# Strassen's algorithm for nine of eleven K-block pairs of the FFN down projection

## The chip, the core and the metric

The kernel runs on one core of a Trainium2 chip. The metric is the device time of one execution in microseconds (us); the kernel before took 1108.36 us, the median of three runs (1108.16 to 1108.46). Five engines matter: TensorE (PE, with its weight loads as PEld) multiplies, VectorE (DVE), ScalarE (ACT) and GpSimd (POOL) work element by element, SyncE (SP) issues the DMAs. SBUF is the on-chip memory of 128 partitions; TensorE writes its results to PSUM, eight banks of 128 x 512 fp32.

## The reference

Two layers of an encoder on 256 tokens, D = 1024, in fp32. Each layer has an FFN, an attention and gating block, and another FFN. Cut to what matters here:

```
def swiglu(x, w_gate, w_up, w_down):
    return (jax.nn.silu(x @ w_gate) * (x @ w_up)) @ w_down

for l in range(DEPTH):                       # DEPTH = 2
    x = x + 0.5 * swiglu(rms_norm(x, ffn1_norm[l]), ffn1_w_gate[l], ffn1_w_up[l], ffn1_w_down[l])
    ...                                      # attention, gates, w_out
    x = x + 0.5 * swiglu(rms_norm(x, ffn2_norm[l]), ffn2_w_gate[l], ffn2_w_up[l], ffn2_w_down[l])
```

The hidden width is 2816, so the down projection multiplies 256 x 2816 by 2816 x 1024, four times in all.

## The kernel before

**Matmuls in three parts.** TensorE is given fp32 numbers in a rounded form (fp32r). So that nothing is lost, each operand is split into a rounded part and the rest: `hi = round(a)` by a copy on ScalarE, `lo = a - hi` by a subtraction on VectorE (`split_to`, lines 176 and 177; for weights the same in `load`, lines 133 and 134, into wh and wl). A product of two blocks is then three matmuls of 512 columns, `three` (lines 162 to 164): hi by hi, hi by lo, lo by hi. This text calls three such matmuls one product.

**Weights.** All weights come through one helper. `load` takes a `raw` buffer of 128 x 1024 (4 of them), issues a DMA of 512 KB on the SP queue, and splits the buffer into wh and wl (RING = 6 slots each). A slot comes free when TensorE has used it in its last product, and a raw buffer when both halves of the split have read it.

**The FFN** (`ffn`) is two stages. Gate/up: eleven chunks c of 256 hidden columns; each chunk loads four pieces of weights and, for each of the two token halves t (128 tokens each), `project` makes eight products into one PSUM bank; Silu on ScalarE (line 323) and a product on VectorE (hh, line 325) make 128 x 256 of the hidden layer. `turn` transposes it on TensorE in 128 x 128 blocks (line 305), and splits the transposed blocks of a chunk from PSUM into hi and lo. `turn` isn't called at once: `defer` and `tick` keep a count of products, and a deferred step is issued when its due count comes (H_LAG = 7.9 for `turn`), or earlier if someone needs it.

Down: `out_rows` runs over the K blocks (128 hidden columns each, 22 in all, two to a chunk). Each loads one row block of w_down, 128 x 1024, and makes four products, one for each token half t and column half d, into four PSUM banks that accumulate over all of K (tags pt, po, and sc twice). So a pair of K blocks, one chunk c, costs eight products. The last four row blocks are one group: there the order is t, then d, then the block, so that banks end one after the other; as each ends, line 292 adds half of it to x, and `after` defers the next norm's transposes of that quarter by NORM_LAG = 4 products. The norm's power (rsqrt, line 168) runs on GpSimd.

**Order.** TensorE's order is the order in which the program is written, with the deferred steps in their places. The order on the other engines is a planner's: it models the program in time ahead of the launch and takes on each engine what is ready, earlier program steps first. On the chip each engine then takes its own list in order.

GpSimd also works in the attention stage: line 443 scales 128 x 512 scores, line 537 adds a mask to a bias.

Of the kernel before, what the change touches and what calls it, by code (L numbers as in the profile page):

```python
# [11 lines left out]
F32 = mybir.dt.float32  # L12
F32R = mybir.dt.float32r
I32 = mybir.dt.int32
BF16 = mybir.dt.bfloat16
AF = mybir.ActivationFunctionType
ALU = mybir.AluOpType
# [4 lines left out]
P = 128  # L22
# [3 lines left out]
FF = 2816  # L26
T = S // P
KD = D // P
FC = 256
NFC = FF // FC  # L30
# [11 lines left out]
RAW = 4  # L42
# [4 lines left out]
FMAX = 3.0e38  # L47
IN_W = 4352
HEAD = 128


@with_exitstack
def hybrid_encoder(ctx, tc, x, w_gu1, w_d1, w_in, b_gate, qk_gain, rpb, sink, t5,
                   w_bna, w_bsw, w_out, w_gu2, w_d2, c_mask, c_hot, c_band, out):
    nc = tc.nc

    const = ctx.enter_context(tc.tile_pool(name="const", bufs=1))
    ring = ctx.enter_context(tc.tile_pool(name="ring", bufs=1))
    act = ctx.enter_context(tc.tile_pool(name="act", bufs=1))
    small = ctx.enter_context(tc.tile_pool(name="small", bufs=4))  # L60
    ps_g = ctx.enter_context(tc.tile_pool(name="ps_g", bufs=2, space=PSUM))
    ps_acc = ctx.enter_context(tc.tile_pool(name="ps_acc", bufs=1, space=PSUM))
    ps_tp = ctx.enter_context(tc.tile_pool(name="ps_tp", bufs=2, space=PSUM))
# [6 lines left out]

    wide = act.tile([P, HEAD + D], F32, name="x0", tag="x0")
    gain = wide[:, :3 * L * KD].rearrange("p (n k) -> p n k", n=3 * L)
    xs = [wide[:, HEAD:], act.tile([P, D], F32, name="x1", tag="x1")]

    def fetch(t, h):
        if (t, h) == (0, 0):
            nc.sync.dma_start(wide[:, :HEAD + 512], x[:P, :HEAD + 512])
        else:
            nc.sync.dma_start(xs[t][:, h * 512:(h + 1) * 512],
                              x[t * P:(t + 1) * P, HEAD + h * 512:HEAD + (h + 1) * 512])  # L80

    fetch(0, 0)

    ident = const.tile([P, P], F32, name="ident")
# [33 lines left out]
    def linked(engine, emit):  # L118
        with ExitStack() as order:
            if engine in chain:  # L120
                order.enter_context(tc.issue_after(chain[engine].ins))
            inst = emit()
        if chain:
            chain[engine] = inst
        return inst

    def load(src, nk, n, tag="raw"):
        raw = ring.tile([P, 2, 512], F32, name="raw", tag="raw", bufs=RAW)
        wh = ring.tile([P, 2, 512], F32R, name="wh", tag="wh", bufs=RING)
        wl = ring.tile([P, 2, 512], F32R, name="wl", tag="wl", bufs=RING)  # L130
        r, h, lo = (w[:, :nk, :n] for w in (raw, wh, wl))
        nc.sync.dma_start(r, src)
        linked("act", lambda: nc.scalar.activation(h, r, AF.Copy))  # L133
        linked("dve", lambda: nc.vector.tensor_tensor(lo, r, h.bitcast(F32), ALU.subtract))  # L134
        return wh, wl

    def columns(w, l, c0, n, nk=KD):
        return [load(w[l, 2 * i * P:(2 * i + 2) * P, c0:c0 + n].rearrange("(k p) n -> p k n", p=P), 2, n)
                for i in range(nk // 2)]

    def rows(w, l, k):
        return load(w[l, k * P:(k + 1) * P, :].rearrange("p (h n) -> p h n", h=2), 2, 512)
# [4 lines left out]
    def defer(lag, key, fn):  # L147
        later.append((now[0] + lag, len(later), key, fn))
        later.sort(key=lambda e: e[0])

    def need(*keys):
        for e in [e for e in later if e[2] in keys]:
            later.remove(e)
            e[3]()

    def tick(cost):
        now[0] += cost
        while later and later[0][0] <= now[0]:
            later.pop(0)[3]()

    def three(ps, xh, xl, wh, wl, first, last):
        nc.tensor.matmul(ps, xh, wh, start=first, stop=False)  # L162
        nc.tensor.matmul(ps, xh, wl, start=False, stop=False)  # L163
        nc.tensor.matmul(ps, xl, wh, start=False, stop=last)  # L164
# [10 lines left out]
    def split_to(hi, lo, src):  # L175
        linked("act", lambda: nc.scalar.activation(hi, src, AF.Copy))
        linked("dve", lambda: nc.vector.tensor_tensor(lo, src, hi.bitcast(F32), ALU.subtract))  # L177
# [39 lines left out]
    def opening(w, l):  # L217
        def piece(i, c=0):
            return load(w[l, 2 * i * P:(2 * i + 2) * P, c * 512:(c + 1) * 512].rearrange("(k p) n -> p k n", p=P),
                        2, 512)  # L220
# [43 lines left out]
    def project(t, pieces, n):  # L264
        ps = ps_g.tile([P, 512], F32, name="g", tag="g")
        for k in range(KD):
            need(("norm", t, k // 4))
            xh, xl = xT[t]
            wh, wl = pieces[k // 2]
            three(ps[:, :n], xh[:, k, :], xl[:, k, :], wh[:, k % 2, :n], wl[:, k % 2, :n], k == 0, k == KD - 1)  # L270
            tick(n / 512)
        return ps

    ACC = ((("pt", 1), ("po", 1)), (("sc", 2), ("sc", 2)))

    def out_rows(get, nk, w, l, groups, scale, after):
        acc = [[ps_acc.tile([P, 512], F32, name="acc", tag=tag, bufs=n) for tag, n in pair] for pair in ACC]
        k0 = 0
        for g in (*[1] * (nk - sum(groups)), *groups):
            pieces = [(k, *rows(w, l, k)) for k in range(k0, k0 + g)]  # L280
            k0 += g
            order = [(d, p) for d in range(2) for p in pieces]
            if k0 < nk:
                order.sort(key=lambda e: e[1][0])
            for t in range(T):
                for d, (k, wh, wl) in order:
                    xh, xl = get(t, k)
                    three(acc[t][d], xh, xl, wh[:, d, :], wl[:, d, :], k == 0, k == nk - 1)
                    tick(1)
                    if k == nk - 1:  # L290
                        xd = xs[t][:, d * 512:(d + 1) * 512]
                        nc.vector.scalar_tensor_tensor(xd, acc[t][d], scale, xd, op0=ALU.mult, op1=ALU.add)  # L292
                        after(t, d)

    def ffn(l, n, w_gu, w_d, after):
        with tc.tile_pool(name="ffn", bufs=1) as fp:
            hs = {}
            tps = {}

            def turn(c, t, hh):  # L300
                if t == 0:
                    tps[c] = ps_tp.tile([P, 2, 2, P], F32, name="tp", tag="tp")
                tp = tps[c]
                for i in range(2):
                    nc.tensor.transpose(tp[:, i, t, :], hh[:, i * P:(i + 1) * P], ident)  # L305
                if t == T - 1:
                    hi = fp.tile([P, 2, 2, P], F32R, name="hi", tag="hi", bufs=NFC)
                    lo = fp.tile([P, 2, 2, P], F32R, name="lo", tag="lo", bufs=NFC)
                    split_to(hi, lo, tp)
                    hs[c] = (hi, lo)  # L310

            for c in range(NFC):
                first = n == 0 and c == 0
                if first:
                    both, second = opening(w_gu, l)
                elif n == 0 and c == 1:
                    pieces = second
                else:
                    pieces = columns(w_gu, l, c * 512, 512)
                for t in range(T):  # L320
                    ps = both[t] if first else project(t, pieces, 512)
                    sg = fp.tile([P, FC], F32, name="sg", tag="sg", bufs=2)
                    nc.scalar.activation(sg, ps[:, :FC], AF.Silu, scale=rstd[t])  # L323
                    hh = fp.tile([P, FC], F32, name="hh", tag="hh", bufs=2)
                    nc.vector.scalar_tensor_tensor(hh, ps[:, FC:], rstd[t], sg, op0=ALU.mult, op1=ALU.mult)  # L325
                    defer(H_LAG, ("h", c), lambda c=c, t=t, hh=hh: turn(c, t, hh))

            def get(t, k):
                need(("h", k // 2))
                return [h[:, k % 2, t, :] for h in hs[k // 2]]  # L330

            out_rows(get, FF // P, w_d, l, (4,), 0.5, after)

    vec_d = dram.tile([NH, 511], F32, name="vec_d")

# [13 lines left out]
    def mix(l, n, after):  # L349
        with tc.tile_pool(name="mix", bufs=1) as mp:  # L350
# [204 lines left out]
            for token in ORDER.split():  # L555
                if token[0] == "a":
                    it, h = next(heads)
# [51 lines left out]
            def get(t, k):  # L609
                need(("merge", t, k // 4))  # L610
                return [m[:, k, :] for m in mT[t]]

            out_rows(get, KD, w_out, l, (4, 4), 0.5, after)

    def store(t, d):
        cols = slice(d * 512, (d + 1) * 512)
# [6 lines left out]
    for l in range(L):  # L623
        ffn(l, 3 * l, w_gu1, w_d1, soon(3 * l + 1))
        mix(l, 3 * l + 1, soon(3 * l + 2))
        ffn(l, 3 * l + 2, w_gu2, w_d2, soon(3 * l + 3) if l + 1 < L else store)
# [67 lines left out]
```

## Time and profile before

| | |
|---|---|
| median of three runs | 1108.36 us |
| the profiled execution | 1108.37 us, of which the span from the first to the last instruction is 1106.5 us |
| TensorE, busy | 1096.3 us, 99% |
| VectorE, busy | 700.5 us, 63% |
| ScalarE, busy | 600.4 us, 54% |
| GpSimd, busy | 103.9 us, 9% |
| granted clock of TensorE | 0.999 on average |

Lines of the profile name an instruction by its source line, engine and operation, then what it writes and reads by the program's names (`wl<-raw,wh`), then shapes as partitions x elements, the number of such instructions, their busy time in us and the mean duration of one in ns, and the idle time of the engine ahead of them with what ended it. A matmul's recorded duration overlaps its neighbours', so a pace is read from starts. Engines' lists of semaphore waits carry a q (DVEq, POOLq). The view of one line or one tile gives shortest, median and longest duration. A timeline gives start and duration in us from the start of the span.

### The profile page before, as it was taken

The numbers are of one execution on the slowest core, as the hardware profiler recorded it, in microseconds if no ns is written. First come the engines' busy times: TensorE is split into PE (matmuls) and PEld (weight loads), VectorE is DVE, ScalarE is ACT, GpSimd is POOL, SyncE is SP. The second block draws the span as 40 slices with busy tenths as digits, with TensorE's granted clock in tenths as the row PEclk, the third lists the DMA queues.
The fourth block names the chain that finished last, engine by engine and source line by source line (L and its number), as shares of the span: only waits on it lengthen the run. The fifth ranks groups of instructions, "written<-read, shape, count | busy, mean of one in ns | idle before, by whom it ended". The sixth has DMA issues, their size and how long they took to land.

```text
span 1106.5 us, 14361 instructions
## 1 busy us (share of the span) xinstructions
PE 1096.3 (99%) x5223; PEld 906.1 (82%) x5223; DVE 700.5 (63%) x987; ACT 600.4 (54%) x914; POOL 103.9 (9%) x101
## 2 busy tenths in 40 slices
PE   9999999999999999999999999999999999999998
PEld 7788888888888888888888888888888888888887
DVE  6655644888887655564475565457888767555542
ACT  6544543788764554454364544347877546454431
POOL 1000000143420000000000000003434000000000
PEclk9999999999999999999999999999999999999999
DMA  7665565765655556556656556647565555646561
GB/s 238 227 188 192 175 212 165 214 189 150 192 183 154 186 175 193 187 176 213 181 156 209 168 187 208 194 119 240 183 190 184 166 171 163 209 161 195 203 192 57
DMA packets 95399, 203.23 MB, mean 184 GB/s; under 512 B 7200, under 2 KB 13376, under 8 KB 95328
## 3 DMA queue, kind: packets, MB, share of 16 engines
q1 hardware_dynamic: 95104, 202.17, 57.7%
q8 instruction: 41, 0.67, 0.3%
q0 software_dynamic: 224, 0.14, 0.1%
q14 instruction: 30, 0.25, 0.1%
HBM read 201.22 MB, written 1.06 MB: 183 GB/s over the span
## 4 chain that ended last, share of the span: by engine, by line
PE 90%; DVE 4%; ACT 3%; issue 2%; DMA 1%; ACTq 0%; DVEq 0%
PE g L162 19%; PE g L164 19%; PE g L163 18%; PE acc L164 9%; PE acc L162 9%; PE acc L163 9%; PE tp L305 2%; DVE wl L134 2%; ACT wh L133 1%; PE tp L193 1%; PE pt L451 1%; PE sc L430 1%; PE g L229 1%; PE po L465 1%; PE br L163 1%
## 5 line engine op out<-in xcount | busy, mean ns | idle before, releaser
L134 DVE TENSOR_TENSOR wl<-raw,wh 128x1024 fp32r<-128x1024 f32 (+1 forms) x368 | 447.0, 1219 | 196.5 <-ACT wh L133 182.7
L133 ACT ACTIVATE wh<-raw 128x1024 fp32r<-128x1024 f32 (+1 forms) x368 | 383.6, 1049 | 209.9 <-PE acc L164 125.2
L162 PE MATMUL g<-wh,xh 128*128 128x512 f32 (+1 forms) x976 | 390.2, 400 | 0.0
L164 PE MATMUL g<-wh,xl 128*128 128x512 f32 (+1 forms) x976 | 379.4, 389 | 0.0
L163 PE MATMUL g<-wl,xh 128*128 128x512 f32 (+1 forms) x976 | 377.8, 387 | 0.4 <-DVE wl L134 0.4
L164 PEld LDWEIGHTS g<-wh,xl 128*128 128x128 f32 x976 | 183.4, 188 | 40.5 <-DVE xl L177 1.3
L163 PEld LDWEIGHTS g<-wl,xh 128*128 128x128 f32 x976 | 184.2, 189 | 31.9 <-DVE wl L134 0.8
L162 PEld LDWEIGHTS g<-wh,xh 128*128 128x128 f32 x976 | 183.7, 188 | 31.5 <-issue 0.9
L323 ACT ACTIVATE sg<-g,rs_y 128x256 f32<-128x256 f32 x88 | 41.7, 474 | 181.6 <-PE g L164 181.4
L162 PE MATMUL acc<-wh,hi 128*128 128x512 f32 x352 | 138.5, 394 | 0.0
L164 PE MATMUL acc<-wh,lo 128*128 128x512 f32 x352 | 137.3, 390 | 0.0
L163 PE MATMUL acc<-wl,hi 128*128 128x512 f32 x352 | 137.1, 389 | 0.0
L325 DVE SCALAR_TENSOR_TENSOR hh<-g,rs_y,sg 128x256 f32<-128x256 f32 x88 | 42.3, 481 | 139.4 <-ACT sg L323 139.4
L164 PEld LDWEIGHTS acc<-wh,lo 128*128 128x128 f32 x352 | 66.1, 188 | 13.9
L163 PEld LDWEIGHTS acc<-wl,hi 128*128 128x128 f32 x352 | 66.2, 188 | 13.4
L162 PEld LDWEIGHTS acc<-wh,hi 128*128 128x128 f32 x352 | 66.1, 188 | 13.3
L168 POOL TENSOR_TENSOR rs_y<-ms,mhalf 128x1 f32<-128x1 f32 x12 | 7.2, 600 | 654.6 <-DVE ms L214 647.4
L443 POOL TENSOR_TENSOR S<-S,sm 128x512 f32<-128x512 f32 x32 | 37.1, 1159 | 71.7 <-DVE sm L442 45.3
L436 ACT ACTIVATE S<-S,mx 128x256 f32<-128x256 f32 x64 | 31.8, 498 | 7.5 <-DVE mx L433 7.4
L305 PEld LDWEIGHTS tp<-ident,hh 128*128 128x128 f32 x176 | 24.6, 140 | 11.3
L292 DVE SCALAR_TENSOR_TENSOR x<-acc,x 128x512 f32<-128x512 f32 x24 | 16.6, 690 | 26.6 <-PE acc L164 26.6
L305 PE MATMUL tp<-ident,hh 128*128 128x128 f32 x176 | 33.3, 271 | 0.0
(133 smaller groups left out, 925.8 us busy)
## 6 DMA issues: line engine op xcount, KB each, us to landing
raw<-in_w_gu SPq DMA_DIRECT2D x176, 512.0 KB, 4.6
raw<-in_w_d SPq DMA_DIRECT2D x88, 512.0 KB, 3.7
raw<-in_w_in SPq DMA_DIRECT2D x64, 512.0 KB, 4.5
raw<-in_w_out SPq DMA_DIRECT2D x16, 512.0 KB, 3.5
bb<-in_b_gate SPq DMA_DIRECT2D x16, 256.0 KB, 3.5
raw<-in_w_bsw SPq DMA_DIRECT2D x8, 512.0 KB, 4.1
raw<-in_w_bna SPq DMA_DIRECT2D x8, 512.0 KB, 3.5
t5b<-vec_d SPq DMA_DIRECT2D x16, 192.0 KB, 3.5
```

What stands on the lines that cost most here:

```text
L133: linked("act", lambda: nc.scalar.activation(h, r, AF.Copy))
L134: linked("dve", lambda: nc.vector.tensor_tensor(lo, r, h.bitcast(F32), ALU.subtract))
L162: nc.tensor.matmul(ps, xh, wh, start=first, stop=False)
L163: nc.tensor.matmul(ps, xh, wl, start=False, stop=False)
L164: nc.tensor.matmul(ps, xl, wh, start=False, stop=last)
L193: nc.tensor.transpose(tp[:, i, :], xs[t][:, k * P:(k + 1) * P], ident)
L292: nc.vector.scalar_tensor_tensor(xd, acc[t][d], scale, xd, op0=ALU.mult, op1=ALU.add)
L305: nc.tensor.transpose(tp[:, i, t, :], hh[:, i * P:(i + 1) * P], ident)
L323: nc.scalar.activation(sg, ps[:, :FC], AF.Silu, scale=rstd[t])
L325: nc.vector.scalar_tensor_tensor(hh, ps[:, FC:], rstd[t], sg, op0=ALU.mult, op1=ALU.mult)
L436: nc.scalar.activation(S_[:, t, :], S_[:, t, :], AF.Exp, bias=mx[:, t:t + 1], scale=-1.0, accum_out=sm[:, t:t + 1])
L443: nc.gpsimd.tensor_tensor(S_, S_, sm.unsqueeze(2).to_broadcast([P, T, S]), ALU.mult)
```

## The change

The 256 tokens are two halves, the 1024 output columns are two halves, and a pair of K blocks is two halves: for each pair the down projection is a 2 x 2 by 2 x 2 block product. The change computes it for the first nine pairs (NS = 9) with seven block products, by the Winograd form of Strassen's algorithm, and keeps the last two pairs (four row blocks) as they were.

- `turn` copies the four transposed blocks of a chunk from PSUM to SBUF on ScalarE (tile a), makes three sums and differences that the algorithm needs and one on the way to them on GpSimd (128 x 128 each), and splits seven blocks from SBUF where four were split from PSUM. The last two chunks stay as before.
- `sevens(c)` loads the two row blocks of a pair, the second into a buffer of its own (`odd`, 3 of them). It splits one corner of 512 columns, the whole second row block, and two tiles u and v of 1024 columns with the differences of weight blocks; those are four subtractions of 128 x 512 on GpSimd, where the second of u feeds the first of v, which feeds the second. u, v and a share four buffers (`sums`). Corner, low, us and vs are the seven right-hand operands; low, us and vs take ring slots, the corner has buffers of its own.
- `products()` accumulates the seven products over the nine pairs in seven PSUM banks. Those of products 2, 3 and 4 go on as accumulators of three of the four output blocks; 1, 5, 6 and 7 are combined by `plus` on VectorE into the parts that the blocks share, three of which GpSimd adds to x and one VectorE.
- `out_rows` then runs over the last four row blocks only, with the accumulators it is given, and takes a new bank for the one that it isn't given.

Cut to its core (`parts` is the splitting half of `load`; `load` itself, and the call of `out_rows` for w_out, do the same as before):

```
+NS = 9
...
+    def parts(r, nk=2, n=512):
         wh = ring.tile([P, 2, 512], F32R, name="wh", tag="wh", bufs=RING)
         wl = ring.tile([P, 2, 512], F32R, name="wl", tag="wl", bufs=RING)
+        split_to(wh[:, :nk, :n], wl[:, :nk, :n], r)
+        return wh, wl
...
             for t in range(T):
                 for d, (k, wh, wl) in order:
+                    first = acc[t][d] is None
+                    if first:
+                        acc[t][d] = out_bank(t, d)
                     xh, xl = get(t, k)
-                    three(acc[t][d], xh, xl, wh[:, d, :], wl[:, d, :], k == 0, k == nk - 1)
+                    three(acc[t][d], xh, xl, wh[:, d, :], wl[:, d, :], first, k == nk - 1)
...
+                if m == 7:
+                    a = fp.tile([P, 8, P], F32, name="a", tag="sums", bufs=4)
+                    nc.scalar.activation(a[:, :4, :], tp, AF.Copy)
+                    for to, x, y, op in ((4, 0, 3, ALU.add), (6, 1, 0, ALU.subtract), (5, 4, 1, ALU.subtract),
+                                         (7, 2, 5, ALU.subtract)):
+                        nc.gpsimd.tensor_tensor(a[:, to, :], a[:, x, :], a[:, y, :], op)
+                    split_to(hi, lo, a[:, 1:, :])
+                else:
                     split_to(hi, lo, tp)
...
+            def sevens(c):
+                r0 = ring.tile([P, 2, 512], F32, name="raw", tag="raw", bufs=RAW)
+                r1 = fp.tile([P, 2, 512], F32, name="odd", tag="odd", bufs=3)
+                for i, r in enumerate((r0, r1)):
+                    k = 2 * c + i
+                    nc.sync.dma_start(r, w_d[l, k * P:(k + 1) * P, :].rearrange("p (h n) -> p h n", h=2))
+                corner = [fp.tile([P, 512], F32R, name=f"c{p}", tag=f"c{p}", bufs=2) for p in "hl"]
+                split_to(*corner, r0[:, 0, :])
+                low = parts(r1)
+                u = fp.tile([P, 2, 512], F32, name="u", tag="sums", bufs=4)
+                v = fp.tile([P, 2, 512], F32, name="v", tag="sums", bufs=4)
+                sub = lambda to, x, y: nc.gpsimd.tensor_tensor(to, x, y, ALU.subtract)
+                sub(u[:, 0, :], r1[:, 1, :], r0[:, 1, :])
+                sub(u[:, 1, :], r0[:, 1, :], r0[:, 0, :])
+                us = parts(u)
+                sub(v[:, 0, :], r1[:, 1, :], u[:, 1, :])
+                sub(v[:, 1, :], r1[:, 0, :], v[:, 0, :])
+                vs = parts(v)
+                half = lambda pair, i: [p[:, i, :] for p in pair]
+                return (("1", 0, corner), ("2", 1, half(low, 0)), ("3", 6, half(low, 1)), ("7", 5, half(us, 0)),
+                        ("5", 3, half(us, 1)), ("6", 4, half(vs, 0)), ("4", 2, half(vs, 1)))
+
+            def products():
+                acc = {"1": ps_g.tile([P, 512], F32, name="g", tag="g"), "2": out_bank(0, 0), "3": out_bank(0, 1),
+                       "4": out_bank(1, 0), "5": ps_tp.tile([P, 512], F32, name="tp", tag="tp"),
+                       "6": ps_g.tile([P, 512], F32, name="g", tag="g"), "7": out_bank(1, 1)}
+                for c in range(NS):
+                    for name, slot, (wh, wl) in sevens(c):
+                        three(acc[name], *[h[:, slot, :] for h in hs[c]], wh, wl, c == 0,
+                              c == NS - 1 and name in "1567")
+                        tick(1)
...
+                nc.scalar.activation(p1[:, 0, :], acc["1"], AF.Copy, scale=0.5)
...
+                u2 = plus(p1[:, 1, :], "6", p1[:, 0, :])
+                u3 = plus(p16[:, 0, :], "7", u2)
+                u4 = plus(p16[:, 1, :], "5", u2)
+                u5 = plus(ends[:, 0, :], "5", u3)
+                for (t, d), u in (((1, 0), u3), ((0, 1), u4), ((1, 1), u5)):
+                    xd = xs[t][:, d * 512:(d + 1) * 512]
+                    nc.gpsimd.tensor_tensor(xd, xd, u, ALU.add)
+                plus(xs[0][:, :512], "1", xs[0][:, :512])
+                return [[acc["2"], acc["3"]], [acc["4"], None]]
...
-            out_rows(get, FF // P, w_d, l, (4,), 0.5, after)
+            out_rows(get, products(), 2 * NS, FF // P, w_d, l, (FF // P - 2 * NS,), 0.5, after)
```

More of the change, by code (lines that the diff above doesn't have):

```diff
@@ L125, in linked, with load @@
         return inst
-    def load(src, nk, n, tag="raw"):
-        raw = ring.tile([P, 2, 512], F32, name="raw", tag="raw", bufs=RAW)
+    def parts(r, nk=2, n=512):
         wh = ring.tile([P, 2, 512], F32R, name="wh", tag="wh", bufs=RING)
         wl = ring.tile([P, 2, 512], F32R, name="wl", tag="wl", bufs=RING)
-        r, h, lo = (w[:, :nk, :n] for w in (raw, wh, wl))
+        split_to(wh[:, :nk, :n], wl[:, :nk, :n], r)
+        return wh, wl
+    def load(src, nk, n):
+        raw = ring.tile([P, 2, 512], F32, name="raw", tag="raw", bufs=RAW)
+        r = raw[:, :nk, :n]
         nc.sync.dma_start(r, src)
-        linked("act", lambda: nc.scalar.activation(h, r, AF.Copy))
-        linked("dve", lambda: nc.vector.tensor_tensor(lo, r, h.bitcast(F32), ALU.subtract))
-        return wh, wl
+        return parts(r, nk, n)
     def columns(w, l, c0, n, nk=KD):
@@ L274, in hybrid_encoder, with out_bank, out_rows @@
     ACC = ((("pt", 1), ("po", 1)), (("sc", 2), ("sc", 2)))
[L276 to L281, printed above, removed]
+    def out_bank(t, d):
+        tag, n = ACC[t][d]
+        return ps_acc.tile([P, 512], F32, name="acc", tag=tag, bufs=n)
+    def out_rows(get, acc, k0, nk, w, l, groups, scale, after):
+        k1 = k0
+        for g in groups:
+            pieces = [(k, *rows(w, l, k)) for k in range(k1, k1 + g)]
+            k1 += g
             order = [(d, p) for d in range(2) for p in pieces]
-            if k0 < nk:
+            if g == 1:
                 order.sort(key=lambda e: e[1][0])
@@ L298, in ffn @@
             tps = {}
+            SLOT = ((1, 2), (0, 3))
             def turn(c, t, hh):
                 if t == 0:
-                    tps[c] = ps_tp.tile([P, 2, 2, P], F32, name="tp", tag="tp")
+                    tps[c] = ps_tp.tile([P, 4, P], F32, name="tp", tag="tp")
                 tp = tps[c]
                 for i in range(2):
[L305 to L308, printed above, removed]
-                    split_to(hi, lo, tp)
-                    hs[c] = (hi, lo)
+                    nc.tensor.transpose(tp[:, SLOT[t][i], :], hh[:, i * P:(i + 1) * P], ident)
+                if t < T - 1:
+                    return
+                m = 7 if c < NS else 4
+                hi = fp.tile([P, m, P], F32R, name=f"hi{m}", tag=f"hi{m}", bufs=NS if m == 7 else NFC - NS)
+                lo = fp.tile([P, m, P], F32R, name=f"lo{m}", tag=f"lo{m}", bufs=NS if m == 7 else NFC - NS)
+                if m == 7:
[6 more added lines that the diff above has]
+                else:
+                    split_to(hi, lo, tp)
+                hs[c] = (hi, lo)
@@ new lines, in get @@
+            def get(t, k):
+                need(("h", k // 2))
+                return [h[:, SLOT[t][k % 2], :] for h in hs[k // 2]]
+            def sevens(c):
[19 more added lines that the diff above has]
+                        ("5", 3, half(us, 1)), ("6", 4, half(vs, 0)), ("4", 2, half(vs, 1)))
@@ new lines, in products, with plus @@
+            def products():
[7 more added lines that the diff above has]
+                        tick(1)
+                p1, p16 = [fp.tile([P, 2, 512], F32, name=n, tag="sums", bufs=4) for n in ("p1", "p16")]
+                ends = fp.tile([P, 2, 512], F32, name="ends", tag="sums", bufs=4)
+                nc.scalar.activation(p1[:, 0, :], acc["1"], AF.Copy, scale=0.5)
+                def plus(to, name, x):
+                    nc.vector.scalar_tensor_tensor(to, acc[name], 0.5, x, op0=ALU.mult, op1=ALU.add)
+                    return to
+                u2 = plus(p1[:, 1, :], "6", p1[:, 0, :])
[7 more added lines that the diff above has]
+                return [[acc["2"], acc["3"]], [acc["4"], None]]
@@ L326, in ffn @@
                     defer(H_LAG, ("h", c), lambda c=c, t=t, hh=hh: turn(c, t, hh))
-            def get(t, k):
-                need(("h", k // 2))
-                return [h[:, k % 2, t, :] for h in hs[k // 2]]
-            out_rows(get, FF // P, w_d, l, (4,), 0.5, after)
+            out_rows(get, products(), 2 * NS, FF // P, w_d, l, (FF // P - 2 * NS,), 0.5, after)
     vec_d = dram.tile([NH, 511], F32, name="vec_d")
@@ L611, in get @@
                 return [m[:, k, :] for m in mT[t]]
-            out_rows(get, KD, w_out, l, (4, 4), 0.5, after)
+            out_rows(get, [[None] * 2 for _ in range(T)], 0, KD, w_out, l, (4, 4), 0.5, after)
     def store(t, d):
```

## The prediction

> **What bounds the kernel now.** I read the page first, its busy rows and the chain.
>
> ```profile
> span 1106.5 us, 14361 instructions
> ...
> PE 1096.3 (99%) x5223; PEld 906.1 (82%) x5223; DVE 700.5 (63%) x987; ACT 600.4 (54%) x914; POOL 103.9 (9%) x101
> ...
> PE 90%; DVE 4%; ACT 3%; issue 2%; DMA 1%; ACTq 0%; DVEq 0%
> ```
>
> TensorE is busy for 99% of the span and is 90% of the chain that ended last; GpSimd is nearly free. So time comes from fewer matmuls, as long as nobody else becomes late. Whether that holds must be read in the stage itself, so next the table by stretches: ten chunks of a gate/up stage, then the down projection behind it (layer 0, second FFN).
>
> ```profile
> core 0: us, PE busy (x) PEld busy (x) DVE busy (x) ACT busy (x) POOL busy (x), PEclk, DMA share, GB/s
> 385.60:495.90 110.30, 110.30 (x504) 90.47 (x503) 62.03 (x68) 54.33 (x68) 0.00 (x0) 1.00 0.56 183
> 495.90:557.30 61.40, 61.40 (x279) 50.74 (x278) 30.45 (x31) 25.09 (x29) 0.55 (x1) 1.00 0.60 187
> ```
>
> In the down projection TensorE has no gap, at a granted clock of 1.00, and VectorE works half the time. The view of the tile acc in that stretch gives its length and shows what holds the splits back:
>
> ```profile
> L162 PE MATMUL acc<-wh,hi x88: 389/389/478, 495.9 to 556.5; 128*128 128x512 f32 x88
> ...
> L164 PE MATMUL acc<-wh,lo x88: 389/389/399, 496.5 to 556.9; 128*128 128x512 f32 x88
> ...
>   ACT wh L133: 30.5, 19
> ```
>
> 264 matmuls, that is 88 products of three, start from 495.9 to 556.9, 61.0 us, so 61.0 / 88 = 0.693 us a product (the 0.39 us of a row overlap their neighbours). The last row is ScalarE waiting 30.5 us for TensorE: the six ring slots are full, and splitting goes at TensorE's pace. The run-ahead is a ring's worth and no more.
>
> **What the change takes away.** Nine pairs of K blocks cost 7 products each instead of 8: nine products per FFN, 9 x 0.693 = 6.2 us, over four FFNs 24.9 us. Transposes stay as many, DMAs too (22 of 512 KB per FFN on the same SP queue; only the buffer of every second one differs).
>
> **What it adds, per pair, in the down projection.** The durations, from the groups kept apart by shape, the view of line 134 in the stretch above, and the views of lines 443 and 537:
>
> ```profile
> L133 ACT ACTIVATE wh<-raw 128x1024 fp32r<-128x1024 f32 x360 | 379.0, 1058 | 208.4 <-PE acc L164 125.2 <-PE g L164 68.3 <-PE br L164 8.7
> ...
> L134 DVE TENSOR_TENSOR wl<-raw,wh 128x512 fp32r<-128x512 f32 x8 | 5.3, 686 | 1.1 <-ACT wh L133 1.1
> ...
> L133 ACT ACTIVATE wh<-raw 128x512 fp32r<-128x512 f32 x8 | 4.8, 624 | 1.5 <-PE g L164 1.5
> ```
>
> ```profile
> L134 DVE TENSOR_TENSOR wl<-raw,wh x21: 1224/1226/1227, 495.7 to 556.4; 128x1024 fp32r<-128x1024 f32 x21
> ```
>
> ```profile
> L443 POOL TENSOR_TENSOR S<-S,sm x32: 1039/1040/1880, 235.6 to 865.5; 128x512 f32<-128x512 f32 x32
> ```
>
> ```profile
> L537 POOL TENSOR_TENSOR b<-t,mask x16: 1185/1198/2057, 249.5 to 850.7; 128x512 f32<-128x512 f32 x16
> ```
>
> Instead of two splits of 1024 there are three and one of 512: VectorE 3 x 1.23 + 0.69 = 4.38 us, ScalarE 3 x 1.06 + 0.62 = 3.80 us. GpSimd gets four subtractions of 128x512. The trace has none with two dense inputs; the nearest are line 443 (one dense, one broadcast input) at an undisturbed 1.04 and line 537 (two odd patterns) at 1.19. I take 1.04, 4.16 us a pair, and keep 1.19 for the range. TensorE needs 7 x 0.693 = 4.85 us a pair. Each engine by itself would fit.
>
> But 1040 to 1880 is a large spread for one instruction. The timeline of the attention stage, VectorE and GpSimd each at two places, shows why:
>
> ```profile
> 256.59 1.99 DVE L134 TENSOR_TENSOR wl<-raw,wh 128x1024 fp32r<-128x1024 f32 x1
> ```
>
> ```profile
> 256.46 1.04 POOL L443 TENSOR_TENSOR S<-S,sm 128x512 f32<-128x512 f32 x1 [2.61 <-ACT ph L176]
> ```
>
> ```profile
> 261.34 1.20 DVE L134 TENSOR_TENSOR wl<-raw,wh 128x1024 fp32r<-128x1024 f32 x1
> ```
>
> ```profile
> 261.59 1.85 POOL L443 TENSOR_TENSOR S<-S,sm 128x512 f32<-128x512 f32 x1 [4.10 <-PE pt L451]
> ```
>
> In the first place GpSimd starts 0.13 us ahead and takes its 1.04 (to 257.50); the split takes 1.99 instead of 1.23 and ends at 258.58, 1.08 after GpSimd. In the second the split is ahead, ends at 262.54 undisturbed, and GpSimd ends at 263.44, 0.90 after it. They do not share, they take turns: one split then costs 1.08 us behind the other engine, one GpSimd operation 0.90, as the start-up hides in the other's turn. It concerns the operand's place, not VectorE as such. This subtraction reads one operand from PSUM and is not held up beside a line 443 at work from 295.87 to 296.91:
>
> ```profile
> 296.33 0.68 DVE L177 TENSOR_TENSOR pl<-pt,ph 128x512 fp32r<-128x512 f32 x1
> ```
>
> ```profile
> 295.87 1.04 POOL L443 TENSOR_TENSOR S<-S,sm 128x512 f32<-128x512 f32 x1 [0.49 <-DVE sm L442]
> ```
>
> All of the change's weight splits read both operands from SBUF, and all its differences on GpSimd do. So the pair's price is a sum, not a maximum: 4 x 0.90 + 3 x 1.08 + 0.54 (half a split) = 7.38 us, against 4.85 on TensorE.
>
> The Trainium skill, "SBUF — State Buffer", section "Who interferes with whom", has this as a rule that speaks against the change: a VectorE instruction with two SBUF inputs and a GpSimd instruction that reads SBUF exclude each other, and "the other **fully blocks** (not throttle)". The trace agrees, and has the hand-over cheaper than two whole instructions (1.08 and 0.90 instead of 1.23 and 1.04).
>
> Another page of the Trainium skill prices the subtraction itself: "GPSIMD Engine Reference", section "Elementwise — side-by-side cycle accounting", gives about 2.6 cycles an element at 1.2 GHz, by which I estimate 1.11 us for 512 elements; put whole in place of 0.90, 24 turns a stage and four stages, it would add 20 us to the sum. Line 443 ended 0.90 after the hand-over, so the sum goes by the trace.
>
> **The stage, summed.** When TensorE starts on the products, part is done already. The last gate/up unit frees its four ring slots one by one, so VectorE is through pair 0 and half of pair 1; GpSimd, with four buffers for its differences, is through pairs 0 to 2. From some 0.5 us into the stage, VectorE has 34 splits ahead of the last group: two of pair 1, four for each of pairs 2 to 8, and the group's four row blocks; 27 of them are whole and 7 half. GpSimd has 6 x 4 = 24 subtractions. I let them alternate while both have work and let VectorE finish alone: 24 x 0.90 + 19 x 1.08 + 5 x 0.54 + 8 x 1.23 + 2 x 0.69 = 56.0 us. VectorE also has the last chunk's hh and transposed split in there, which hold nobody up but take its time:
>
> ```profile
> L325 DVE SCALAR_TENSOR_TENSOR hh<-g,rs_y,sg 128x256 f32<-128x256 f32 x88 | 42.3, 481 | 139.4 <-ACT sg L323 139.4
> ...
> L177 DVE TENSOR_TENSOR lo<-tp,hi 128x512 fp32r<-128x512 f32 x44 | 30.4, 691 | 0.1
> ...
> L292 DVE SCALAR_TENSOR_TENSOR x<-acc,x 128x512 f32<-128x512 f32 x24 | 16.6, 690 | 26.6 <-PE acc L164 26.6
> ```
>
> 0.48 + 0.69 = 1.17. The fourth row block is ready at 0.5 + 56.0 + 1.17 = 57.7 us; TensorE then has that product and twelve more, 13 x 0.693 = 9.0, so the stage lasts 66.7 us instead of 61.0: 5.7 more, in four FFNs 22.8.
>
> Behind it, five combinations of products on VectorE (nearest row: line 292, 0.69) stand ahead of the final addition to x, which the next norm's transposes need: combinations and addition end 6 x 0.69 = 4.1 us after the fourth block, the transposes are due after five products, 3.5 us. That is 0.7 us, in the three FFNs with a norm behind them 2.1. With TensorE as the bound the combinations would have run during the last group and cost nothing. GpSimd's three additions to x stand ahead of the norm's power on its queue, but that one needs the final x anyway.
>
> New waits: a split of differences waits on VectorE for ScalarE's half, which waits for GpSimd; queued behind it are the next pair's splits of plain weights, and TensorE waits for all. Bounds: every turn at the hand-over price, and no wait of the norm, gives a stage of 65.2 and +17 us; every instruction at its whole 1.23, 0.69 and 1.04 gives 73.7 and +53; with 1.19 for GpSimd +67. I stay near the lower, as both queues are mostly full.
>
> In gate/up the change adds per pair an ACT copy (512 elements), a split of 896 instead of 512 elements, and four GpSimd operations of 128 elements (between the 0.29 us of a 128x128 copy, row below, and 1.04 each). VectorE has 110.30 - 62.03 = 48 us free in ten chunks, 4.8 each; 0.4 us for the larger split plus four turns at under 1.04 stay below that, ScalarE has 5.6 free. I cost it at nothing; uncovered it would be 36 x 0.4 us and up.
>
> ```profile
> L383 POOL COPY kn<-kn 128x128 f32<-128x128 f32 x4 | 1.2, 292 | 0.5 <-DVE kn L361 0.3 <-ACT sqT L376 0.3
> ```
>
> Sum: the profiled execution took 1108.37 us (span 1106.5), the median of the runs is 1108.36. 1108.4 + 22.8 + 2.1 = 1133 us.
>
> **Rivals.** (A) the forecast: the taking of turns becomes the bound, 1133, between 1112 and 1175.
> (B) The pairs do not overlap. One pair's own chain is four subtractions, a copy and a split, 4 x 1.04 + 1.06 + 1.23 = 6.45, plus two other splits' turns inside it, 2.16: 8.6 us. If the order on the queues lets no second pair in, seven pairs take 60.2 and the fourth row block comes at 0.5 + 2.2 + 60.2 + 4.9 + 1.2 = 69 us; stage 78, +17 x 4 + 2: 1178. For it: in-order queues and a chain that crosses three engines twice. Against: buffers for two pairs.
> (C) The other side: the two engines do not exclude each other for dense operands, or only in part. Then 4.85 us of TensorE covers 4.38, 4.16 and 3.80, and the whole 24.9 us come: 1083.5. It decides at about 6.6 us a pair, where the stage is 61.0 again. Against: the rows above, with hand-overs exact to 0.02 us; for: no row has a dense subtraction.
> (D) TensorE's gaps lower its granted clock, say to half: a pair then costs 2 x 4.85 = 9.7, more than the 7.4, and 79 products at twice 0.693 are 109.5 us a stage: 1108 + 4 x 48.5 = 1302. The Trainium skill's "TensorE: Matmul & The Clock Gate", section "The HAM clock gate (the "warmup" mystery)", states a half clock after an idle window of about 3.4 us. Against: some 2.5 us of idleness a pair, in several pieces, and a granted clock of 1.00 in the stretches above.
>
> **How the numbers follow.** A 0.75, B 0.13, C 0.09, D 0.03. About 0.2%, 2.2 us, is what a measurement can tell from no change. A lies wholly beyond it but for its lowest end (0.02 for no change); B and D are slower, C faster: 0.09 / 0.02 / 0.89. The range leaves out C and D and A's and B's ends: 1112 (some 3.3 us of turns a stage more done ahead than I counted, 13 below the 1125 of the lower bound) to 1180 (B).
>
> **What would show it.** Down stages of about 67 us with TensorE waiting some 12 us in each for VectorE's wl, mostly in the later pairs; 128x1024 splits there near 2 us instead of 1.23 while GpSimd works, its subtractions near 1.9, never both progressing; gate/up stages unchanged at 11.0 us a chunk; clock 1.00. Wrong if TensorE stays without gaps (C), if GpSimd and VectorE idle together while TensorE waits (B), or if the granted clock falls (D).

## The result and the profile after

The changed kernel took 1192.41 us (median of four runs, 1191.51 to 1193.17) beside 1108.41 us of the kernel before: 1.0754 times as long, interval 1.0735 to 1.0773. The forecast of slower was right; its size was not: 84 us more instead of 25, and outside the range.

The busy rows of the page after, and its clock and chain:

```profile
span 1191.2 us, 14822 instructions
...
PE 1108.6 (93%) x5115; PEld 888.5 (75%) x5115; DVE 907.7 (76%) x1079; ACT 673.1 (57%) x1026; POOL 480.4 (40%) x401
...
PE 58%; DVE 23%; issue 9%; POOL 4%; ACT 4%; DMA 3%; DVEq 0%; ACTq 0%; POOLq 0%
```

108 matmuls fewer (5223 to 5115), as meant, and yet 85 us more span. The chain that ended last was TensorE for 90%; now it is TensorE for 58% and VectorE for 23%. The table of the four down stages after, with the columns of the prediction's table, tells where:

```profile
137.30:220.40 83.10, 65.33 (x249) 47.41 (x248) 79.06 (x55) 38.92 (x48) 63.67 (x33) 0.94 0.36 109
518.90:602.30 83.40, 64.33 (x249) 46.17 (x249) 79.21 (x55) 38.84 (x48) 63.73 (x33) 0.96 0.37 116
729.30:811.00 81.70, 63.70 (x250) 46.03 (x249) 79.25 (x55) 39.20 (x48) 63.72 (x33) 0.96 0.35 111
1109.70:1187.30 77.60, 62.67 (x241) 45.46 (x240) 73.26 (x47) 32.90 (x38) 62.26 (x32) 0.96 0.29 93
```

From the start of the first to the start of the last matmul the stages last 82.9, 83.2, 81.5 and 77.4 us, where they lasted 61.0, 61.0, 61.0 and 60.0: 82 of the 84 us are here, and gate/up and attention are as long as before within a us each. In the first row VectorE is busy 79.06 of 83.10 us, with 55 instructions; before, 31 took it 30.45. A good part of this is waiting inside instructions: 25 splits of 1024 and 7 of 512 that read both operands from SBUF last 64.6 us there as recorded, where 25 x 1.23 + 7 x 0.69 = 35.6 us is what they take undisturbed. The timeline of the first stage, VectorE and GpSimd over one pair of K blocks:

```profile
153.82 1.77 DVE L180 TENSOR_TENSOR cl<-raw,ch 128x512 fp32r<-128x512 f32 x1
155.52 0.68 DVE L180 TENSOR_TENSOR lo<-tp,hi 128x512 fp32r<-128x512 f32 x1
156.12 1.72 DVE L180 TENSOR_TENSOR wl<-odd,wh 128x1024 fp32r<-128x1024 f32 x1
157.76 2.31 DVE L180 TENSOR_TENSOR wl<-u,wh 128x1024 fp32r<-128x1024 f32 x1
159.99 2.30 DVE L180 TENSOR_TENSOR wl<-v,wh 128x1024 fp32r<-128x1024 f32 x1
162.22 1.77 DVE L180 TENSOR_TENSOR cl<-raw,ch 128x512 fp32r<-128x512 f32 x1
```

```profile
155.00 1.75 POOL L348 TENSOR_TENSOR u<-odd,raw 128x512 f32<-128x512 f32 x1
156.72 2.27 POOL L348 TENSOR_TENSOR u<-raw 128x512 f32<-128x512 f32 x1
159.06 2.15 POOL L348 TENSOR_TENSOR v<-odd,u 128x512 f32<-128x512 f32 x1
161.29 2.15 POOL L348 TENSOR_TENSOR v<-odd,v 128x512 f32<-128x512 f32 x1
```

Read the ends. GpSimd ends at 156.75, 158.99, 161.21 and 163.44; the wl splits of odd, u and v end at 157.84, 160.07 and 162.29, each 1.08 or 1.09 after GpSimd, and GpSimd 1.14 to 1.15 after each of them. The corner's split comes every 8.40 us (153.82, 162.22): this is the price of a pair. The engines take turns, as forecast, but the pair costs 8.4 us instead of 7.38, because GpSimd's turn lasts 1.15 and not 0.90. The view of the subtractions' line:

```profile
L348 POOL TENSOR_TENSOR u<-odd,raw x36: 1288/1743/2282, 120.4 to 1158.8; 128x512 f32<-128x512 f32 x36
L348 POOL TENSOR_TENSOR v<-odd,v x36: 1282/2140/2274, 132.7 to 1167.3; 128x512 f32<-128x512 f32 x36
```

The shortest ones, which nothing disturbs, show what a subtraction with two dense operands takes: 1.28 us, and not the 1.04 of line 443, whose second operand is broadcast.

TensorE also stands still once at the start of a stage, for the last chunk's hh, and once near the end, for the addition to x that the norm reads. From the list of waits in the first stage:

```profile
PEld g L165 <- DVE hh L399: 3.2, 1, 3.2
PEld tp L196 <- DVE x L301: 3.2, 1, 3.2
```

### The profile page after: what moved, and what is told of

It reads as the page before. It is cut to its first block, busy times and chain, and to the rows that moved or that the text cites. A ratio compares the mean times of both kernels' runs of the same rounds, so it can differ in the third digit from the quotient of the medians.

```text
span 1191.2 us, 14822 instructions
## 1 busy us (share of the span) xinstructions
PE 1108.6 (93%) x5115; PEld 888.5 (75%) x5115; DVE 907.7 (76%) x1079; ACT 673.1 (57%) x1026; POOL 480.4 (40%) x401
## 3 DMA queue, kind: packets, MB, share of 16 engines
HBM read 201.22 MB, written 1.06 MB: 170 GB/s over the span
## 4 chain that ended last, share of the span: by engine, by line
PE 58%; DVE 23%; issue 9%; POOL 4%; ACT 4%; DMA 3%; DVEq 0%; ACTq 0%; POOLq 0%
DVE wl L180 16%; PE g L165 15%; PE g L167 15%; PE g L166 15%; DVE cl L180 3%; PE acc L166 2%; PE acc L167 2%; PE acc L165 2%; ACT wh L179 2%; POOL u L348 2%; PE tp L316 1%; POOL v L348 1%; DVE lo L180 1%; DMA raw<-in_w_gu 1%; PE tp L196 1%
## 5 line engine op out<-in xcount | busy, mean ns | idle before, releaser
L180 DVE TENSOR_TENSOR wl<-raw,wh 128x1024 fp32r<-128x1024 f32 (+1 forms) x296 | 361.7, 1233 | 98.9 <-ACT wh L179 94.5
L179 ACT ACTIVATE wh<-raw 128x1024 fp32r<-128x1024 f32 (+1 forms) x296 | 304.3, 1042 | 95.3 <-PE g L167 48.7
L327 POOL TENSOR_TENSOR a<-a 128x128 f32<-128x128 f32 x144 | 69.3, 501 | 299.3 <-ACT a L324 288.3
L165 PE MATMUL acc<-wh,hi 128*128 128x512 f32 x208 | 86.0, 414 | 0.0
L167 PE MATMUL acc<-wh,lo 128*128 128x512 f32 x208 | 84.7, 407 | 0.0
L348 POOL TENSOR_TENSOR u<-odd,raw 128x512 f32<-128x512 f32 x36 | 69.3, 1925 | 37.2 <-issue 18.9
L348 POOL TENSOR_TENSOR u<-raw 128x512 f32<-128x512 f32 x36 | 77.3, 2147 | 0.0
L180 DVE TENSOR_TENSOR wl<-u,wh 128x1024 fp32r<-128x1024 f32 x36 | 77.0, 2140 | 0.0
L180 DVE TENSOR_TENSOR wl<-odd,wh 128x1024 fp32r<-128x1024 f32 x36 | 76.2, 2118 | 0.0
L348 POOL TENSOR_TENSOR v<-odd,u 128x512 f32<-128x512 f32 x36 | 75.5, 2097 | 1.6
```

The costliest lines, as they stand in the source:

```text
L327: nc.gpsimd.tensor_tensor(a[:, to, :], a[:, x, :], a[:, y, :], op)
L348: sub = lambda to, x, y: nc.gpsimd.tensor_tensor(to, x, y, ALU.subtract)
```

## The experiments

The theory after the result: the second SBUF operand of VectorE and GpSimd's reads exclude each other; a pair's price is the sum of the turns, 4 x 1.15 + 3 x 1.08 + 0.54, and this sum, not any single stall, sets the stage's end. The rivals: (1) TensorE's separate stalls, with the half clock that follows them, are losses of their own, some 10 us a stage; (2) the pair's chain over GpSimd, ScalarE and VectorE sets the pace, whoever holds the operand. Runs with a ratio and an interval were made four times; the others, one run each, show differences far above the 1.7 us by which the runs of the changed kernel differ, or are called no gain.

**Subtractions on VectorE.**

```
-                sub = lambda to, x, y: nc.gpsimd.tensor_tensor(to, x, y, ALU.subtract)
+                sub = lambda to, x, y: nc.vector.tensor_tensor(to, x, y, ALU.subtract)
```

> The four subtractions of a pair go from GpSimd to VectorE; all else as in the changed kernel, whose pairs cost 8.4 us in the steady part. Theory (taking turns at the second SBUF operand: 4 x 1.16 + 3 x 1.08 + 0.54 = 8.4): with one engine there are no turns, VectorE alone needs 3 x 1.14 + 5 x 0.60 = 6.4 us a pair, more than TensorE's 4.85, so some 2 us less on six or seven pairs a stage: 1140 us, between 1125 and 1155. Rival 1 (the stage is long because of TensorE's separate stalls, for hh, for the norm and at the half clock, some 10 us a stage): these stay, VectorE is busier than before, so no gain: 1185 to 1200.

1133.78 us. The groups of this run inside its second down stage:

```profile
L180 DVE TENSOR_TENSOR wl<-u,wh 128x1024 fp32r<-128x1024 f32 x8 | 9.8, 1219 | 0.0
...
L348 DVE TENSOR_TENSOR u<-raw 128x512 f32<-128x512 f32 x6 | 4.1, 684 | 0.0
```

Splits are back at 1.22 us, and VectorE does a subtraction in 0.68 where GpSimd held it up for 1.15. One engine doing all the work is 59 us faster than two that exclude each other. The first three pairs run at TensorE's pace (4.9, 5.0, 4.8 us), the later ones do not (4.8 to 7.0). TensorE's wait for hh is gone in this run too, so by itself it does not exclude rival 1; the run with hh first, below, does that.

**Nothing read by GpSimd.**

```
-                sub(u[:, 0, :], r1[:, 1, :], r0[:, 1, :])
-                sub(u[:, 1, :], r0[:, 1, :], r0[:, 0, :])
+                nc.gpsimd.memset(u, 0.5)
+                nc.gpsimd.memset(u, 0.25)
                 us = parts(u)
...                                              # v likewise
```

> The four subtractions on GpSimd are replaced by four memsets of 1024 elements, so u and v hold constants and the products with them are not the reference's; the buffers, the order of steps and GpSimd's place in each pair's chain stay, but GpSimd reads nothing from SBUF in the down stages. Theory (turns): the splits fall back to 1.23 us, TensorE sets the pair at 4.85 us, and the kernel takes 1083 to 1100 us, less than before the change. Rival 2 (a pair's chain over three engines sets the pace, whoever holds the port): the chain is nearly as long, so pairs stay above 7 us and the kernel above 1150.

1085.50 us, the 24.9 us of removed products less 2. The views of line 180 in the second down stage and of the tile v:

```profile
L180 DVE TENSOR_TENSOR wl<-v,wh x8: 1224/1226/1227, 492.0 to 525.5; 128x1024 fp32r<-128x1024 f32 x8
```

```profile
L352 POOL MEMSET v<- x36: 950/958/962, 111.9 to 1053.1; 128x1024 f32 x36
```

The splits keep their 1.23 us beside a GpSimd that writes 0.96 us at a time, and every pair costs 4.8 to 5.0. The chain over three engines is there all the same, shorter by four times 0.32 and without GpSimd's wait for the loaded rows: one pair's own chain is still 4 x 0.96 + 1.06 + 1.23 = 6.1 us, and it doesn't set the pace. Rival 2 is out. Three whole splits and a half one a pair, and GpSimd's writing, fit under TensorE: what is too much is GpSimd's reading.

**A broadcast second operand.**

```
+                sub = lambda to, x, y: nc.gpsimd.tensor_tensor(to, x, y[:, :1].to_broadcast([P, 512]), ALU.subtract)
```

> The second operand of the four subtractions is one broadcast column, as in the attention stage's line that gave the price in the prediction, so u and v hold other differences than the reference needs. Theory (turns, with the dense subtraction at 1.28 us undisturbed and 1.16 in a turn being the mis-sized term): GpSimd's turn falls to 0.92, a pair to 7.4, and over seven pairs in four stages 28 us go: 1164, between 1155 and 1173. If the second operand's pattern makes no difference to GpSimd: 1190 to 1195, and the long turn comes from the contention itself.

1158.97 us. The view of its subtractions, and VectorE's timeline from one corner to the next:

```profile
L348 POOL TENSOR_TENSOR v<-odd,u x36: 1034/1902/2022, 124.4 to 1130.2; 128x512 f32<-128x512 f32 x36
```

```profile
540.06 1.52 DVE L180 TENSOR_TENSOR cl<-raw,ch 128x512 fp32r<-128x512 f32 x1
541.51 2.06 DVE L180 TENSOR_TENSOR wl<-odd,wh 128x1024 fp32r<-128x1024 f32 x1
543.49 2.06 DVE L180 TENSOR_TENSOR wl<-u,wh 128x1024 fp32r<-128x1024 f32 x1
545.47 2.06 DVE L180 TENSOR_TENSOR wl<-v,wh 128x1024 fp32r<-128x1024 f32 x1
547.45 1.52 DVE L180 TENSOR_TENSOR cl<-raw,ch 128x512 fp32r<-128x512 f32 x1
```

Undisturbed 1.03 us, and a pair every 7.39 us (540.06 to 547.45): the prediction's 7.38, at its own price. So the sum of turns of one pair was built rightly, and only the price of one operation was taken from the wrong row. That price, with what follows from it elsewhere in the kernel, is worth 33 of the 59 us by which the forecast was short.

**hh ahead of the second pair's splits on VectorE.**

```
+                    if behind is not None:
+                        order.enter_context(tc.issue_after(behind.ins))
                     low = parts(r1)
```

> VectorE's queue is changed at one place: the second pair's splits stand behind the last chunk's hh, so that hh no longer waits for two splits of 2.3 us and TensorE does not stall 3.2 us for a PSUM bank in the first pair. Theory (turns set the stage's end): the time is given back at the later pairs, which wait longer; 1186 to 1195, a gain of 0 to 6. Rival 1 (the stalls add up): 3.2 us and 1.7 us of half clock behind it are gained in each of four stages: 1172, between 1168 and 1177.

1189.22 us, 1.0719 of the kernel before (1.0701 to 1.0737). The first pair now takes 4.9 us instead of 8.5, and the stages still last 80.8, 81.1, 80.9 and 78.6: the later pairs wait longer. Rival 1's 20 us are not there, only 3.

**The end of the stage.** The combinations and the first addition to x ahead of the next stage's splits:

```
+            for inst in held:
+                order.enter_context(tc.issue_after(inst.ins))
             linked("dve", lambda: nc.vector.tensor_tensor(lo, src, hi.bitcast(F32), ALU.subtract))
```

> VectorE's queue is changed at the end of each stage: the five combinations of products and the first final addition to x stand ahead of the next stage's weight splits. In the changed kernel the norm's first transposes wait 3.2 us for that addition and TensorE then runs 3.4 us at half clock, 1.7 us lost, in the three FFNs with a norm behind them. Theory (this end comes on top, since nothing after it makes up for it): 3 x 4.5 us are gained: 1179, between 1175 and 1184. If the next stage's splits, now later, stall its first products instead: 1186 to 1193.

1193.23 us, no gain: my expectation was wrong, and its second branch, 0.2 us below this, came nearest. The stages are shorter, 79.8, 79.8, 79.7 and 78.6 us, but the stretch from the first to the second of them, with attention in it, is 303.4 instead of 298.7 us. Part of it shows at this place of the run's timeline, a wait of TensorE that the changed kernel does not have there, in the attention stage's transposes and not at the next stage's first products:

```profile
243.87 0.85 PE L454 MATMUL tp<-ident_r,qs 128*128 128x128 f32 x8 [1.75 <-DVE hv L439]
```

**The chunk's sums on VectorE.**

```
-                        nc.gpsimd.tensor_tensor(a[:, to, :], a[:, x, :], a[:, y, :], op)
+                        nc.vector.tensor_tensor(a[:, to, :], a[:, x, :], a[:, y, :], op)
```

> The four 128-element sums of a chunk in the gate/up stage go from GpSimd to VectorE; the weights' subtractions stay on GpSimd. In the changed kernel they share GpSimd's queue with the first pairs' subtractions, ScalarE waits 7.4 us for the last sum ahead of splits, and VectorE enters the stage with two whole splits of pairs 0 and 1 undone (2 x 2.24 us) that the prediction had counted as done. Theory (the lost lead is that queueing): the lead comes back, 4 x 4.5 us are gained: 1174, between 1169 and 1181. If the lead is set by the ring slots alone: 1187 to 1194.

1195.41 us: wrong as well, and above both branches. The lead does come back, the first pairs take 4.9 to 5.4 us and the four stages together 14 us less, but TensorE loses them in gate/up just ahead, where a split comes late. (All four sums are left-hand operands of products; none is only on the way to another, as the section on the change has it.) The timeline of TensorE before the second down stage:

```profile
513.28 0.79 PE L166 MATMUL g<-wl,xh 128*128 128x512 f32 x1 [3.30 <-DVE wl L180]
```

Three attempts to mend a single stall, three times the time came back elsewhere. This fits a shared resource without slack: reordering leaves the turns around a down stage about as many and as long, and only fewer or shorter turns helped, as in the first three runs. It is a reading of the three runs, and no run isolates it.

**Fewer pairs.** If that is so, seven products pay where the extra work has room. Three pairs, and the subtractions on VectorE:

```
-NS = 9
+NS = 3
...
-            out_rows(get, products(), 2 * NS, FF // P, w_d, l, (FF // P - 2 * NS,), 0.5, after)
+            out_rows(get, products(), 2 * NS, FF // P, w_d, l, (*[1] * (FF // P - 2 * NS - 4), 4), 0.5, after)
```

> Only the first three pairs in seven products, the other eight as before the change, and the subtractions on VectorE. Theory (a pair's splits and subtractions, 6.4 us on VectorE, can be done ahead for some three pairs, as the first three pairs at 4.9 us in the run with the subtractions on VectorE show; a plain pair needs 2.4 of its 5.5 us): nine... three products less a stage, 4 x 3 x 0.693 = 8.3 us, are gained against the kernel before: 1100, between 1099 and 1105. If the combinations or the extra work cost TensorE time whatever the number of pairs: 1106 to 1112.

1102.84 us, 0.9948 of the kernel before (0.9932 to 0.9965): 5.3 of the 8.3 us.

**Six pairs with plain ones between them.**

```
+                for c in range(MIXED):
+                    if c not in SEVEN:
...                                                        # plain pair: four products for each row block
+                        continue
                     for name, slot, (wh, wl) in sevens(c):
```

> Six pairs (0, 1, 2, 4, 6, 8) in seven products and five plain ones between and behind them, the subtractions on VectorE, an eighth PSUM bank for the fourth output block. Theory (TensorE stays the bound as long as the splits of any stretch fit: a mixed couple needs 6.4 + 2.4 = 8.8 us of VectorE and 4.85 + 5.54 = 10.4 of TensorE): the six products a stage are gained whole: 1108.5 - 4 x 6 x 0.693 = 1092, between 1090 and 1098. If splits stall TensorE even so (queue order, ring slots): 1100 or more.

1098.47 us, 0.9908 of the kernel before (0.9893 to 0.9922), and 0.5 us past the range that I had written. The second down stage of this run, in the same columns:

```profile
495.30:553.20 57.90, 57.59 (x261) 47.33 (x260) 51.79 (x61) 33.80 (x40) 5.32 (x4) 1.00 0.51 164
```

TensorE has no gap to speak of, VectorE is busy for 51.79 of 57.90 us. The stages last 57.4, 57.4, 57.4 and 55.9 us; together 14.8 us less than before the change; 2.4 are lost ahead of the first one, which starts at 139.0 instead of 136.6, and some 3.5 more in the stretches between. So six products a stage are not gained whole, as the theory had it: outside the down stages the change costs time that the theory put at nothing.

**Seven pairs.** SEVEN = (0, 1, 2, 4, 5, 7, 8).

> As the run with six mixed pairs, with seven (0, 1, 2, 4, 5, 7, 8) and four plain ones. Theory (VectorE's work against TensorE's, stretch by stretch): a plain pair and two others need 2.4 + 2 x 6.4 = 15.2 us of VectorE and 5.54 + 2 x 4.85 = 15.2 of TensorE, so it is just covered; at most one product a stage more is gained, 2.8 us: 1096, between 1094 and 1099. If VectorE has no room left after six: 1100 to 1106.

1097.35 us, 0.9904 (0.9888 to 0.9921). Not told apart from six by these intervals; it has the lowest time of the kernels that leave nothing out, 11 us below the kernel before.

**Six mixed pairs, subtractions on GpSimd.** The lambda of the first experiment turned back.

> The run with six mixed pairs, with the subtractions on GpSimd again. Theory (turns: a seven-product pair takes 8.4 us of the shared operand, a plain one 2.2 to 2.5, a couple 10.8 against TensorE's 10.4, and the first three pairs 25.2 against 14.6 with some 13 us of lead): TensorE waits a few us in the first three pairs, for hh among others, and can't make it up: 1110 to 1126, slower than the kernel before. If GpSimd's help is worth having once plain pairs are mixed in: below 1098, as VectorE has 2.4 us less to do in each of six pairs.

1132.09 us, slower than my 1110 to 1126, and 34 us slower than with VectorE doing them alone. The stages last 66.0, 66.0, 65.8 and 64.4 us, with the first seven products at 8.1 to 9.2 us each time. GpSimd's help is a loss with plain pairs mixed in, too.

## Why the prediction was wrong, point by point

- **Taking turns as the bound: right.** It was read from four rows of the attention stage, and the run with memsets shows it by taking it away: 1085.5 us, within 2 us of the 1083.5 given for rival C, in which nothing excludes anything. (The words quoted from the Trainium skill's "SBUF — State Buffer", section "Who interferes with whom", stand there for VectorE's 2-port modes; of an instruction with two SBUF inputs the section says that it contends with a reading GpSimd, under a rule that calls the shared ports an exclusive lock. That a split and a subtraction exclude each other rests here on the timelines.)
- **"I take 1.04, 4.16 us a pair": this step failed.** The four subtractions read two dense operands; line 443 reads one. Undisturbed 1.28 instead of 1.04, in a turn some 1.16 (8.4 less 3.78, by four) instead of 0.90: 24 x 0.26 = 6.2 us a stage. The upper price that I kept, line 537 at 1.19, was too low as well. By itself this step, 25 us in four stages, would have made the forecast 1158, still inside the range; the next two terms carry the time out of it.
- **"VectorE is through pair 0 and half of pair 1; GpSimd [...] is through pairs 0 to 2": wrong on both engines.** On VectorE, v of pair 0 and the second block of pair 1 came after the stage's start (wl<-odd at 138.78, stage from 137.3). GpSimd was through pairs 0 and 1 only: 28 subtractions start within each of the four stages, where I counted 24, and four more turns of 1.16 are 4.6 us. VectorE's two additional splits, some 1.7 us by the prediction's prices, are nearly set off: hh and the transposed split, which I added with 1.17, read one operand from PSUM and ran inside GpSimd's turns (hh at 143.23, the split at 155.52 in the timeline above). With the 6.2 us of the price, 57.7 + 6.2 + 4.6 = 68.5 us to the last group's fourth row block where I said 57.7; its split ended 68.7 us into the first stage. Why the lead was shorter stays open.
- **"That is 0.7 us" for the norm: too little.** The addition to x stood behind two of the next stage's splits; the norm's transposes waited 3.2 us, and TensorE's clock was halved behind it. The last group, from the fourth row block on, took 14.2 us instead of 9.0. That is 5.2 us more, 4.5 beyond the 0.7. The run that reordered this end had shorter stages and the same time, so in the whole kernel this term does not look like a loss of its own.
- **Stage by stage:** 66.7 + 6.2 for the price + 4.6 for the lead + 5.2 for the end (14.2 less 9.0) = 82.7 us, measured 82.9 in the first stage. In the last stage, which has no norm behind it, 66.7 + 6.2 + 4.6 = 77.5, measured 77.4.
- **hh and the transposed split "hold nobody up": wrong, and nearly harmless.** hh held a PSUM bank that the sixth product needs; mended, 3 of 84 us came back.
- **Gate/up at nothing: right** within a us a stage.
- **Rival B** (pairs that do not overlap) came out nearest in time, 1178, but that is luck, as it was not the cause: subtractions of one pair ran beside splits of another throughout.
- **Rival D** happened in small: nine times 3.4 us at half clock. What these cost by themselves stays open; where TensorE waits for splits afterwards anyway, a slower product should cost nothing, but I did not isolate it.

## What to carry to other kernels

Before work is handed to an idle engine, ask what it shares with the busy one: here GpSimd with 9% load cost more time than VectorE doing its work, because each of its reads stopped a split with two SBUF operands. Where a bound is a sum of turns, price each operation by a row with the same operands, dense or broadcast, and expect a mended stall to come back elsewhere until turns are taken away. An algorithm with fewer matmuls pays for as many blocks as the other engines have room for: with the subtractions on VectorE, three pairs at the start gave 5 us, six mixed with plain ones 10, and nine in a row cost 25. Mixing is argued from the engines' sums; six in a row were not run.

## What the runs showed of the hardware

A GpSimd subtraction of 128 x 512 fp32 took 1.28 us with two dense SBUF operands and 1.03 with one of them broadcast. Beside VectorE subtractions with two SBUF operands both engines alternate without a gap, 2.24 us for one subtraction and one split of 1024; a GpSimd memset of 128 x 1024 (0.96 us) held no split up.

TensorE's granted clock went to half nine times in the changed kernel, for 3.4 us each, during or soon after a stretch of 2.2 to 3.0 us without a matmul. Two of eleven such stretches were not followed by it, and in the run with the subtractions on VectorE one of 3.05 us (to 197.95) was while one of 3.07 us (to 565.62) was not; what decides stays open. A table of the changed kernel: a stall and the half clock behind it, then the 3.4 us behind a stall from 522.61 to 525.39 at full clock. The number behind GpSimd's is the granted clock:

```profile
140.60:143.70 3.10, 0.37 (x2) 0.00 (x0) 3.10 (x4) 2.32 (x3) 3.02 (x2) 1.00 0.45 128
144.70:148.10 3.40, 3.40 (x11) 2.61 (x10) 3.40 (x3) 1.41 (x2) 3.40 (x2) 0.50 0.01 2
525.40:528.80 3.40, 3.40 (x16) 2.78 (x17) 3.40 (x3) 0.46 (x1) 3.32 (x3) 1.00 0.06 23
```
